# Second product of a SwiGLU FFN: seven block products in place of eight for 18 of its 22 tiles, with the gated blocks split early and kept in DRAM

## The chip, the core and the metric

The kernel runs on one core of a Trainium2 chip. Its time is the device time of one execution, in microseconds (us). Before the change the median of three runs is 1400.06 us (1399.25 to 1402.87). The engines that matter here are TensorE (PE in the rows), which multiplies matrices, VectorE (DVE), ScalarE (ACT), GpSimd (POOL) and SyncE (SP). GpSimd and SyncE are used here to issue transfers between SBUF (the memory on the core) and DRAM. PSUM is the small memory that TensorE writes; its banks hold 128 x 512 float32 values each.

## What is computed

A decoder block: attention and convolution branches, then a SwiGLU FFN. Only the FFN is touched:

```python
h2 = rmsnorm(x, norm2_g[l]) * (1.0 + sc2) + sh2
fg, fu = jnp.split(h2 @ w_ffn_in[l], 2, axis=-1)
x = x + gt2 * ((jax.nn.silu(fg) * fu) @ w_ffn_out[l])
return rmsnorm(x, final_g)
```

There are 1024 positions, 1024 channels and 2816 hidden channels, so the hidden side is 22 tiles of 128 channels. Everything is float32. To keep its accuracy on TensorE, each operand is split into a rounded high half and the remainder (the low half), and each product is made of three matmuls: high by high, high by low, low by high.

## The kernel before

**First product** (`h2 @ w_ffn_in`). The class `Pair` (line 1144) takes two hidden tiles at a time, first their gate columns, then their up columns, so that there are 22 pairs. A pair is a 2 x 2 by 2 x 2 block product made as seven products in place of eight (Winograd's form, table `PRODUCTS`): products 0 to 6 use the blocks A11, S1, S2, S4, S3, A12, A22 of the activations, where the S are sums and differences of blocks, and B11, T1, T2, B22, T3, B21, T4 of the weights, where T1 to T4 are differences. One product is 12 matmuls of 128 x 512 (4 tiles of depth, three matmuls each) into one of three PSUM banks: products 0, 2, 4, 6 go on adding into X, 1 and 3 into Z, 5 into Y. Between them the bank is read: after products 0, 1 and 2 ScalarE copies it out (`keep`: `kepta`, `keptc`, `keptb`), after 3, 4, 5 and 6 `out` makes the hidden tile from bank and kept copy, with VectorE for the additions and ScalarE for the silu of a gate pair. The next product into a bank waits until it has been read. There are six such banks, given out in turn.

**Weights.** `prepare` (line 1178) makes one product's weight block: for a T VectorE first takes the difference (`tt`), ScalarE rounds it (high half, `wb` or `wbp`), and VectorE takes the remainder (same tile). The loop at line 1386 prepares up to six products ahead (`LEAD`). In this stretch TensorE, VectorE and ScalarE each keep the order in which the code was written (`in_order`): an instruction that waits holds up everything behind it on its engine.

**Gated tiles.** A finished tile `g` (silu(gate) * up, 128 x 1024) goes to DRAM (`g_d`) by a transfer that GpSimd issues. There are 32 SBUF slots of 128 x 1024 for everything large; 28 hold the split blocks of the activations.

**Second product** (`@ w_ffn_out`). The gated tiles come in groups of 6, 6, 6 and 4 (line 1422). SyncE's queue loads them (`gl`), each is split (ACT 1024 columns, DVE 1024 columns), and for each of 8 output tiles m and each half of the positions the bank `fo` adds 3 matmuls per tile. VectorE then adds it, times a column, to the residual tile `x1r`. The last group of four also makes the final rmsnorm and the output.

Of the kernel before, what the change touches and what calls it, by code (L numbers as in the profile page):

```python
# [16 lines left out]
P = 128  # L17
S = 1024
# [53 lines left out]
LEAD = 6  # L72
CN = ((4, 0), (5, 0), (5, 1), (6, 0), (7, 0))
# [20 lines left out]
def tile_hybrid_block(ctx: ExitStack, tc: tile.TileContext, xT, vecs, cvec, lamv, relb, bsel, bmask, jrev,  # L94
# [793 lines left out]
    with tc.tile_pool(name="ps2", bufs=6, space=bass.MemoryType.PSUM) as ps2, ExitStack() as fxs:  # L888
# [203 lines left out]
        g_d = dp.tile([NFF, P, S], F32, name="g_d")  # L1092
        acts = {}
# [50 lines left out]
        class Pair:  # L1144
# [3 lines left out]

            def __init__(self, i):
                self.i = i  # L1150
                self.up = i % 2 == 1
                self.f = i // 2 * 2
                self.w, self.banks, self.kept = {}, {}, {}

            def load(self):
                self.raw = []
                for n in range(2):
                    if self.up:
                        t = fx[0].tile([P, D], F32, tag="raw", name="rawu", bufs=2)
                    else:  # L1160
                        t = wp.tile([P, D], F32, tag="wraw", name="rawg")
                    nc.sync.dma_start(t, w_fi[self.f + n + (NFF if self.up else 0)])
                    self.raw.append(t)
                (b11, b21), (b12, b22) = ((t[:, :HB], t[:, HB:]) for t in self.raw)
                self.b = dict(B11=b11, B21=b21, B12=b12, B22=b22)

            def source(self, name):
                b = self.b
                if name == "T1":
                    self.t = fx[0].tile([P, S], F32, tag="tt", name="tt", bufs=2)  # L1170
                if name[0] == "T":

                    b[name] = self.t[:, HB:] if name == "T3" else self.t[:, :HB]
# [7 lines left out]
            def high(self, p):  # L1181
# [3 lines left out]
                split_hi(w[:, :HB], src)  # L1185
                return w, src

            def low(self, part):
                w, src = part
                V.tensor_tensor(out=w[:, HB:], in0=src, in1=w[:, :HB].bitcast(F32), op=ALU.subtract)  # L1190

            def product(self, p, part=range(KH)):
                an, bn, x = self.PRODUCTS[p]
                if part[0] == 0:
# [5 lines left out]
                for k in part:  # L1200
                    a = acts[an][k]
                    ks = slice(k * P, (k + 1) * P)
                    ls = slice(HB + k * P, HB + (k + 1) * P)

                    mm3(self.banks[x], w[:, ks], w[:, ls], a[:, :HB], a[:, HB:], first and k == 0, k == KH - 1,
                        skip_group_check=not first)
# [37 lines left out]
            def store(self, n):  # L1244

                f = self.f + n
                if self.up and f < NFF - 2:
                    G.dma_start(g_d[f], hidden[f])
# [6 lines left out]
        nblock = [0]  # L1255

        def weight_block():
            n = nblock[0] % NWB
            nblock[0] += 1
            if n < NWB - 4:  # L1260
# [123 lines left out]
        late = {}  # L1384
        G0 = list(range(NFF - 6, NFF))
        for n, (g, p) in enumerate(order):
            if n < 14:
                continue
            if p == 1 and g.i + 2 < NFF:
# [183 lines left out]
```

## Time and profile before

| | before |
|---|---|
| median of three runs | 1400.06 us |
| profiled execution: its own time | 1404.03 us |
| profiled execution: span from first to last instruction | 1402.2 us |
| TensorE busy | 1360.9 us, 97% |
| VectorE busy | 964.4 us, 69% |
| ScalarE busy | 598.9 us, 43% |
| mean granted TensorE clock | 0.993 |
| moved by DMA | 135.10 MB |

Busy time is the sum over an engine's instructions. Matmuls overlap, so one matmul's own duration is longer than the distance between two starts, and it is the distance that adds up to the time. The chain of waits is followed backwards from the last instruction, at each step to what released it. In a row in order of time the idle time before an instruction stands in brackets with what ended it. In names, `<-` has the output at its left and the inputs at its right; a line such as L107 is that of a helper through which all engines' instructions run.

### The profile page before, as it was taken

Reading aid. Unit: us, or ns where it says so; the run is one execution under the profiler, and the core shown is the slowest. Engines: PE = TensorE matmul, PEld = TensorE weight load, DVE = VectorE, ACT = ScalarE, POOL = GpSimd, SP = SyncE. Lnnn points to the kernel's source line nnn. Section 1 sums busy time; section 2 is a strip of 40 time slices with the busy share of each in tenths; the row PEclk is TensorE's granted clock in tenths of the full one; section 3 lists DMA queues with packets and bytes.
Section 4 is the critical chain, followed back from the end, with each engine's and each line's share of the span. In section 5 each row is a group of like instructions: output and inputs, shape, how many; then the busy total and the mean of one; then the engine's idle time right before and its main releaser. Section 6 shows DMA issues by size and latency. Waiting matters only on the chain.

```text
span 1402.2 us, 15979 instructions
## 1 busy us (share of the span) xinstructions
PE 1360.9 (97%) x6178; PEld 1113.0 (79%) x6178; DVE 964.4 (69%) x1473; ACT 598.9 (43%) x974; POOL 45.3 (3%) x71
## 2 busy tenths in 40 slices
PE   7999999999999999999998999999999999999996
PEld 5678887877788887787766888888888888888886
DVE  7847788899989896887788655656555554434345
ACT  5546666666511115533565333333333332212145
POOL 0000000000000000000000000000000000000004
PEclk9999999999999999999999999999999999999998
DMA  8511011101111123339612222332222335313203
GB/s 296 194 31 34 30 43 30 31 16 38 40 59 46 45 91 105 120 132 324 211 38 103 86 105 98 120 120 91 90 75 78 111 128 191 135 45 113 72 15 121
DMA packets 44270, 135.10 MB, mean 96 GB/s; under 512 B 4857, under 2 KB 7841, under 8 KB 44194
## 3 DMA queue, kind: packets, MB, share of 16 engines
q1 hardware_dynamic: 39458, 118.88, 25.3%
q0 software_dynamic: 4160, 14.68, 3.1%
q8 instruction: 48, 0.79, 0.2%
q10 hardware_dynamic: 576, 0.52, 0.1%
q14 instruction: 28, 0.23, 0.1%
HBM read 115.19 MB, written 18.88 MB: 96 GB/s over the span
## 4 chain that ended last, share of the span: by engine, by line
PE 78%; DVE 9%; ACT 6%; DMA 4%; issue 1%; POOL 1%; SPq 0%; DVEq 0%; ACTq 0%; POOLq 0%
PE fx L107 16%; PE fo L119 16%; PE proj L107 8%; PE fz L107 8%; PE ga L107 5%; PE fy L107 4%; PE gc L107 4%; PE oa L107 3%; PE oc L119 3%; PE vacc L119 2%; DMA ada<-in_w_ada 2%; PE sc L107 2%; PE wo L119 2%; PE av L107 2%; PE wps L107 1%
## 5 line engine op out<-in xcount | busy, mean ns | idle before, releaser
L119 DVE SCALAR_TENSOR_TENSOR x1r<-fo,cols,x1r 128x512 f32<-128x512 f32 (+1 forms) x72 | 49.3, 690 | 119.9 <-PE fo L119 119.6
L119 PE MATMUL fo<-gl,wh_fo 128*128 128x512 f32 x288 | 112.2, 390 | 0.0
L119 PE MATMUL fo<-gh,wl_fo 128*128 128x512 f32 x288 | 112.1, 389 | 0.0
L119 PE MATMUL fo<-gh,wh_fo 128*128 128x512 f32 x288 | 111.9, 389 | 0.0
L107 DVE SCALAR_TENSOR_TENSOR cacc<-u,vec,cacc 128x1022 f32<-128x1022 f32 (+28 forms) x87 | 110.2, 1267 | 2.2
L107 PE MATMUL proj<-hhi,wh_in 128*128 128x512 f32 x239 | 99.3, 416 | 1.7 <-DVE kl L119 1.7
L107 PE MATMUL proj<-hhi,wl_in 128*128 128x512 f32 x240 | 94.9, 395 | 0.0
L107 PE MATMUL proj<-hlo,wh_in 128*128 128x512 f32 x240 | 94.6, 394 | 0.0
L107 PE MATMUL fx<-A,wb 128*128 128x512 f32 x335 | 80.9, 397 | 2.8 <-DVE g L107 2.8
L119 ACT ACTIVATE wh_fo<-wr_fo 128x768 fp32r<-128x768 f32 x24 | 20.3, 847 | 135.9 <-PE fo L119 130.3
L107 PEld LDWEIGHTS fx<-A,wb 128*128 128x128 f32 x335 | 63.9, 191 | 17.3 <-issue 3.7
L107 PE MATMUL fz<-S,wb 128*128 128x512 f32 x312 | 75.4, 390 | 1.6 <-DVE S L107 1.6
L107 PE MATMUL fx<-S,wb 128*128 128x512 f32 x312 | 75.2, 390 | 1.4 <-DVE S L107 1.3
L107 PEld LDWEIGHTS fz<-S,wb 128*128 128x128 f32 x312 | 58.4, 188 | 14.5 <-DVE S L107 2.4
L107 PEld LDWEIGHTS fx<-S,wb 128*128 128x128 f32 x312 | 58.5, 188 | 14.2 <-DVE S L107 1.6
L107 DVE TENSOR_TENSOR wb<-tt,wb 128x512 fp32r<-128x512 f32 x52 | 35.8, 693 | 45.2 <-ACT wb L107 45.1
L119 PEld LDWEIGHTS fo<-gl,wh_fo 128*128 128x128 f32 x288 | 54.1, 188 | 11.7 <-DVE gl L119 0.4
L119 PEld LDWEIGHTS fo<-gh,wh_fo 128*128 128x128 f32 x288 | 54.1, 188 | 11.3
L119 PEld LDWEIGHTS fo<-gh,wl_fo 128*128 128x128 f32 x288 | 54.1, 188 | 11.1
L119 ACT ACTIVATE e<-sc,mn 128x512 f32<-128x512 f32 (+7 forms) x64 | 47.2, 739 | 25.9 <-DVE mn L119 25.0
L107 ACT ACTIVATE wb<-tt 128x512 fp32r<-128x512 f32 x52 | 32.6, 629 | 59.5 <-DVE tt L107 59.3
L107 PEld LDWEIGHTS proj<-hhi,wh_in 128*128 128x128 f32 x239 | 45.7, 191 | 11.3 <-issue 3.6
(324 smaller groups left out, 3364.9 us busy)
## 6 DMA issues: line engine op xcount, KB each, us to landing
ada<-in_w_ada SPq DMA_DIRECT2D x32, 512.0 KB, 4.4
rawu<-in_w_fi SPq DMA_DIRECT2D x22, 512.0 KB, 3.5
rawg<-in_w_fi SPq DMA_DIRECT2D x22, 512.0 KB, 4.3
g_d<-g POOLq DMA_DIRECT2D x20, 512.0 KB, 4.1
gl<-g_d SPq DMA_DIRECT2D x20, 512.0 KB, 5.6
wr_fo<-in_w_fo SPq DMA_DIRECT2D x24, 384.0 KB, 3.1
adac<-in_w_ada SPq DMA_DIRECT2D x16, 512.0 KB, 4.8
wr_wo<-in_w_out SPq DMA_DIRECT2D x16, 512.0 KB, 5.2
```

Source lines behind the costliest of these rows:

```text
L107: self.last = f(*args, **kw)
L119: self.last = self.chain(f, *args, **kw) if self.chain else f(*args, **kw)
```

## The change

18 of the 22 gated tiles (`NST = 9` twos) no longer come into the second product as they are. While the first product goes on, `g_steps` makes from each two tiles the seven left-hand blocks of Winograd's form (A12, A22, A11, S1, S3, S2, S4): it splits each into high and low half in a tile `gst` and lets GpSimd store it in DRAM (`gs_d`). The steps of a two start at product 4 of its up pair and go on one per product, behind the matmuls and ahead of the reading of the bank, to product 3 of the next gate pair; those of the first two stand two per product at the start. In the second product these 18 tiles make three depths of 3 x 2 tiles, for each of which four `Group`s (a subclass of `Pair`, two output tiles each) make seven products of 9 matmuls. Their left-hand blocks are loaded by GpSimd's queue (`gb`, 21 per depth), 3 after each product of the last up pair and, for the later depths, 7 early and the rest as slots fall free. The weight blocks are prepared four products ahead. Each product is read out by VectorE into `x1r`. The four tiles that are left go as the last group did. The `ada2` loads, two in each 14 products, become one.

The core of the diff (the last group's code only moves to the left):

```diff
+LEAD2 = 4
+NST = 9
+GP = 3
+GB = ("A11", "S1", "S2", "S4", "S3", "A12", "A22")
...
-                if self.up and f < NFF - 2:
+                if self.up and f >= 2 * NST:
                     G.dma_start(g_d[f], hidden[f])
+        class Group(Pair):
+            n = GP * P
+            OUT = ((0, 0, "X"), (1, 1, "Z"), (0, 1, "X"), (0, 1, "Z"), (1, 1, "X"), (0, 0, "Y"), (1, 0, "X"))
...
+            def blocks(self, name):
+                return gacts[self.g][name]
+            def evacuate(self, p):
+                hf, n, x = self.OUT[p]
+                t = x1[self.m + n][:, hf_sl(hf)]
+                V.scalar_tensor_tensor(out=t, in0=self.banks[x], scalar=col(5, self.m + n), in1=t, op0=ALU.mult,
+                                       op1=ALU.add)
+        def g_steps(i):
+            a11, a21 = (hidden[2 * i][:, hf_sl(hf)] for hf in range(2))
+            a12, a22 = (hidden[2 * i + 1][:, hf_sl(hf)] for hf in range(2))
+            def put(name, src):
+                t = slot("gst", F32R)
+                split(t[:, :HB], t[:, HB:], src)
+                G.dma_start(gs_d[i * 7 + GB.index(name)], t)
+            def summed(name, out, x, y, op=ALU.subtract):
+                def f():
+                    t = out if out is not None else t2("gs1")
+                    V.tensor_tensor(out=t, in0=x, in1=y, op=op)
+                    put(name, t)
+                return f
+            return [lambda: put("A12", a12), lambda: put("A22", a22), lambda: put("A11", a11),
+                    summed("S1", None, a21, a22, ALU.add), summed("S3", a21, a11, a21), summed("S2", a11, a22, a21),
+                    summed("S4", a12, a12, a11)]
...
+        def fetch_blocks(group, n):
+            while n and wanted and wanted[0][0] == group:
+                n -= 1
+                g, name, k = wanted.pop(0)
+                if g == 1 and GP <= GP * ORDER.index(name) + k < GP + NWB - 6:
+                    t = fx[0].tile([P, D], F32R, tag="wb", name="gbw", bufs=NWB - 4)
+                else:
+                    t = slot("gb", F32R)
+                nc.gpsimd.dma_start(t, gs_d[(g * GP + k) * 7 + GB.index(name)])
+                gacts.setdefault(g, {}).setdefault(name, []).append(t)
...
+        late = g_steps(0)
         for n, (g, p) in enumerate(order):
...
             g.product(p)
+            if first:
+                if g.up and p == 4 and g.i // 2 < NST:
+                    late = g_steps(g.i // 2)
+                for _ in range(2 if n < 18 else 1):
+                    if late:
+                        late.pop(0)()
             g.evacuate(p)
...
+                if i == NFF - 1:
+                    fetch_blocks(0, GP)
+                    if p >= 5:
+                        x1r()
+            else:
+                if i < NFF + 4 and len(x1) < KD:
+                    x1r()
+                if g.m == 2 and p == 0:
+                    fetch_blocks(g.g + 1, 7)
+                elif g.m == KD - 2:
+                    fetch_blocks(g.g + 1, GP)
...
-        groups = [G0] + [list(range(a, b)) for a, b in ((0, 6), (6, 12), (12, 16))]
+        grp = list(range(2 * NST, NFF))
```

VectorE's order in the first product, in the middle of it, from the remainder of the next up pair's B11 to the first addition of the gate pair's product 3; first before the change. `wb` are remainders, `tt` are differences of weights, `g13` is a hidden tile.

```order
L107 TENSOR_TENSOR wb_7298<-rawu_7159,wb_7298 128x512
L107 TENSOR_TENSOR tt_7316<-rawu_7161,rawu_7159 128x512
L107 TENSOR_TENSOR wb_7318<-tt_7316,wb_7318 128x512
L107 ISA ada2_7219,cols_90<-ada2_7219,crow_82,bada_84 128x1024
L107 ISA cols_90 128x1
L107 TENSOR_TENSOR tt_7316<-rawu_7161,tt_7316 128x512
L107 TENSOR_TENSOR wb_7337<-tt_7316,wb_7337 128x512
L107 TENSOR_TENSOR g13_7352<-fz_7301,keptb_7333 128x512
```

The same place now; `g10` and `g11` are the two finished tiles, whose sums (written over them) and remainders (`gst`) stand between:

```order
L112 TENSOR_TENSOR wb_7459<-rawu_7306,wb_7459 128x512
L112 TENSOR_TENSOR g10_7266<-g10_7266 128x512
L112 TENSOR_TENSOR gst_7476<-g10_7266,gst_7476 128x512
L112 TENSOR_TENSOR tt_7482<-rawu_7308,rawu_7306 128x512
L112 TENSOR_TENSOR wb_7484<-tt_7482,wb_7484 128x512
L112 TENSOR_TENSOR g10_7266<-g11_7229,g10_7266 128x512
L112 TENSOR_TENSOR gst_7500<-g10_7266,gst_7500 128x512
L112 TENSOR_TENSOR tt_7482<-rawu_7308,tt_7482 128x512
L112 TENSOR_TENSOR wb_7507<-tt_7482,wb_7507 128x512
L112 TENSOR_TENSOR g11_7229<-g11_7229,g10_7266 128x512
L112 TENSOR_TENSOR gst_7523<-g11_7229,gst_7523 128x512
L112 TENSOR_TENSOR g13_7527<-fz_7462,keptb_7504 128x512
```

Behind each weight block stands a step of the gated tiles, a sum and a remainder, and the addition that reads product 3's bank (`fz`) comes behind all of them.

ScalarE's order at the same place before, from the copy of product 0's bank to the gate's silu:

```order
L107 ACTIVATE kepta_7292<-fx_7279 128x512
L107 ACTIVATE wb_7298<-rawu_7159 128x512
L107 ACTIVATE keptc_7314<-fz_7301 128x512
L107 ACTIVATE wb_7318<-tt_7316 128x512
L107 ACTIVATE keptb_7333<-fx_7279 128x512
L107 ACTIVATE wb_7337<-tt_7316 128x512
L107 ACTIVATE g13_7352<-g13_7352 128x512
```

And now, where the row ahead of `kepta` is the rounding of S1:

```order
L112 ACTIVATE gst_7449<-gs1_7447 128x512
L112 ACTIVATE kepta_7453<-fx_7434 128x512
L112 ACTIVATE wb_7459<-rawu_7306 128x512
L112 ACTIVATE gst_7476<-g10_7266 128x512
L112 ACTIVATE keptc_7480<-fz_7462 128x512
L112 ACTIVATE wb_7484<-tt_7482 128x512
L112 ACTIVATE gst_7500<-g10_7266 128x512
L112 ACTIVATE keptb_7504<-fx_7434 128x512
L112 ACTIVATE wb_7507<-tt_7482 128x512
L112 ACTIVATE gst_7523<-g11_7229 128x512
L112 ACTIVATE g13_7527<-g13_7527 128x512
```

Each copy of a bank (`kepta`, `keptc`, `keptb`) now stands behind the rounding of a gated block (`gst`), which needs the sum that VectorE takes in the same product.

SyncE's queue where the second product starts, before (`gl` gated tiles, `wr_fo` weights, `x1r` the residual):

```order
L177 DMA wr_fo00_8594<-in_w_fo 128x768
L177 DMA wr_fo01_8642<-in_w_fo 128x768
L1410 DMA gl16_8564<-g_d_3193 128x1024
L1410 DMA gl17_8566<-g_d_3193 128x1024
L1410 DMA gl18_8568<-g_d_3193 128x1024
L1410 DMA gl19_8570<-g_d_3193 128x1024
L177 DMA wr_fo02_8690<-in_w_fo 128x768
L177 DMA wr_fo03_8738<-in_w_fo 128x768
L1435 DMA x1r0_8592<-x1_d_3192 128x1024
L1435 DMA x1r1_8640<-x1_d_3192 128x1024
L1435 DMA x1r2_8688<-x1_d_3192 128x1024
```

And now (`rawu` and `rawg` are weights of the first `Group`s):

```order
L1284 DMA rawu_8769<-in_w_fo 128x768
L1284 DMA rawu_8771<-in_w_fo 128x768
L1284 DMA rawg_8964<-in_w_fo 128x768
L1474 DMA x1r0_8888<-x1_d_3192 128x1024
L1474 DMA x1r1_8913<-x1_d_3192 128x1024
L1474 DMA x1r2_8930<-x1_d_3192 128x1024
```

The first load of `x1r` now stands behind the load into `rawg_8964`, whose buffer falls free when the first `Group`'s T3 has been taken.

## Rows read from the trace of the kernel before

**Rows 1.** The page, part 1: busy us of each engine, share of span, instructions.

```profile
PE 1360.9 (97%) x6178; PEld 1113.0 (79%) x6178; DVE 964.4 (69%) x1473; ACT 598.9 (43%) x974; POOL 45.3 (3%) x71
```

**Rows 2.** Chain that ended last: start us, us, what; both products of the FFN.

```profile
844.15 2.72 PE fz L107 x12
...
1143.35 2.72 PE fx L107 x12
1146.08 222.21 PE fo L119 x996
```

**Rows 3.** Page, part 5, one of three alike: busy, mean ns of one, idle before.

```profile
L119 PE MATMUL fo<-gh,wh_fo 128*128 128x512 f32 x288 | 111.9, 389 | 0.0
```

**Rows 4.** Stretch: its us, then busy PE, PEld, DVE, ACT, POOL, PEclk, DMA, GB/s.

```profile
914.24:952.32 38.08, 38.08 (x169) 31.55 (x168) 23.55 (x36) 14.02 (x24) 1.06 (x3) 1.00 0.32 111
```

**Rows 5.** VectorE in order of time, first product: start us, us, instruction [idle before].

```profile
898.39 0.69 DVE L107 TENSOR_TENSOR tt<-rawu,tt 128x512 f32<-128x512 f32 x1
899.84 0.69 DVE L107 TENSOR_TENSOR wbp<-tt,wbp 128x512 fp32r<-128x512 f32 x1 [0.76 <-ACT wbp L107]
902.46 0.69 DVE L107 TENSOR_TENSOR wb<-rawg,wb 128x512 fp32r<-128x512 f32 x1 [1.93 <-ACT wb L107]
903.07 0.68 DVE L107 TENSOR_TENSOR tt<-rawg 128x512 f32<-128x512 f32 x1
...
907.06 0.69 DVE L107 TENSOR_TENSOR tt<-rawg,tt 128x512 f32<-128x512 f32 x1
...
909.47 0.69 DVE L107 TENSOR_TENSOR keptb<-fz,keptb 128x512 f32<-128x512 f32 x1 [0.34 <-PE fz L107]
910.20 0.69 DVE L107 TENSOR_TENSOR g<-keptb,g 128x512 f32<-128x512 f32 x1
```

**Rows 6.** ScalarE in the same stretch.

```profile
899.17 0.63 ACT L107 ACTIVATE wbp<-tt 128x512 fp32r<-128x512 f32 x1
901.31 0.60 ACT L107 ACTIVATE kepta<-fx 128x512 f32<-128x512 f32 x1 [1.51 <-PE fx L107]
901.80 0.62 ACT L107 ACTIVATE wb<-rawg 128x512 fp32r<-128x512 f32 x1
...
907.78 0.63 ACT L107 ACTIVATE wb<-tt 128x512 fp32r<-128x512 f32 x1 [0.43 <-DVE tt L107]
```

**Rows 7.** Chain again, third pair of the first product.

```profile
772.80 3.00 PE fz L107 x12
775.80 3.00 PE fx L107 x12
```

**Rows 8.** Transfers issued from 800 to 1143 us: KB each, median us to landing.

```profile
g_d<-g POOLq DMA_DIRECT2D x18, 512.0 KB, 4.1
...
x1r<-x_d SPq DMA_DIRECT2D x5, 512.0 KB, 6.8
```

**Rows 9.** Tile g_d, stores and loads: duration ns min/median/max; us to landing.

```profile
L1248 POOL DMA_DIRECT2D g_d<-g x20: 531/531/539, 758.8 to 1109.0; - x20
...
DMA to landing us min/median/max: 2.9/4.2/7.9
```

**Rows 10.** Stretches as in rows 4: fullest transfers, then behind the last products.

```profile
625.00:630.00 5.00, 5.00 (x24) 4.14 (x23) 4.41 (x7) 1.60 (x2) 0.73 (x1) 1.00 1.01 395
630.00:635.00 5.00, 5.00 (x24) 4.14 (x23) 4.11 (x8) 1.59 (x2) 0.55 (x1) 1.00 1.01 371
1388.00:1392.00 4.00, 1.51 (x10) 0.94 (x8) 2.65 (x6) 2.95 (x8) 4.00 (x6) 1.00 0.31 109
1392.00:1396.00 4.00, 1.96 (x5) 0.80 (x4) 0.79 (x2) 3.18 (x5) 2.09 (x3) 0.56 0.45 155
```

**Rows 11.** By form, from 1143 us: additions to x1r, splits of 768 columns.

```profile
L119 DVE SCALAR_TENSOR_TENSOR x1r<-fo,cols,x1r 128x512 f32<-128x512 f32 x56 | 42.0, 751 | 116.9 <-PE fo L119 116.7
...
L119 DVE TENSOR_TENSOR wl_fo<-wr_fo,wh_fo 128x768 fp32r<-128x768 f32 x22 | 20.9, 950 | 0.0
...
L119 ACT ACTIVATE wh_fo<-wr_fo 128x768 fp32r<-128x768 f32 x22 | 18.6, 848 | 135.9 <-PE fo L119 130.3 <-issue 5.5
```

More of the change, by code (lines that the diff above doesn't have):

```diff
@@ L1092, in tile_hybrid_block @@
         g_d = dp.tile([NFF, P, S], F32, name="g_d")
+        gs_d = dp.tile([NST * 7, P, S], F32R, name="gs_d")
         acts = {}
@@ L1382, in tile_hybrid_block, with x1r @@
         nprep = 17
-        late = {}
-        G0 = list(range(NFF - 6, NFF))
+        gacts = {}
+        x1 = []
+        ORDER = [a for a, b, x in Pair.PRODUCTS]
+        wanted = [(g, name, k) for g in range(NST // GP) for name in ORDER for k in range(GP)]
+        def fetch_blocks(group, n):
[8 more added lines that the diff above has]
+                gacts.setdefault(g, {}).setdefault(name, []).append(t)
+        def x1r():
+            x1.append(slot(f"x1r{len(x1)}"))
+            nc.sync.dma_start(x1[-1], x1_d[len(x1) - 1])
+        seq = pairs + [Group(i) for i in range(NST // GP * KD // 2)]
+        order += [(g, p) for g in seq[NFF:] for p in range(7)]
+        late = g_steps(0)
         for n, (g, p) in enumerate(order):
@@ new lines, in tile_hybrid_block, with fg, weighted, end @@
+        parts = (slice(0, HB), slice(HB, HB + HB // 2), slice(HB + HB // 2, S))
+        stf, accs, lasts, rest = {}, {}, {}, []
+        def fg(m):
+            return vec[:, O_FG + m:O_FG + m + 1]
+        def weighted(hs, m):
+            return hs != parts[-1] or m < KD - 2
+        def end(hs, engine):
+            sums = [accs[hs]] + (rest if hs == parts[-1] else [])
+            for i, t in enumerate(sums):
+                T.matmul(stf[hs], ones, t, start=(i == 0), stop=(i == len(sums) - 1))
+            r = rstd_from([stf[hs]], 1.0 / D, lasts[hs], fslot)[0]
+            for m in range(KD):
+                t = x1[m][:, hs]
+                if weighted(hs, m):
+                    engine.tensor_tensor(out=t, in0=t, in1=r, op=ALU.mult)
+                else:
+                    V.scalar_tensor_tensor(out=t, in0=t, scalar=fg(m), in1=r, op0=ALU.mult, op1=ALU.mult)
+                (nc.scalar if m % 2 and hs == parts[-1] else nc.sync).dma_start(outT[m][:, hs], t)
@@ new lines, in tile_hybrid_block @@
+        for i, hs in enumerate(parts):
+            nt = hs.stop - hs.start
+            stf[hs] = bankG("stf")[:, 0:nt]
+            one = hs != parts[-1]
+            for m in range(KD):
+                ps = bank("fo")[:, 0:nt]
+                gemm_cols(ps, wl[m], g_acts, hs)
+                if i and m == EP:
+                    end(parts[i - 1], G)
+                t = x1[m][:, hs]
+                V.scalar_tensor_tensor(out=t, in0=ps, scalar=col(5, m), in1=t, op0=ALU.mult, op1=ALU.add)
+                sq = (t2 if m else fslot)("sq")[:, 0:nt]
+                if one or m < KD - 1:
+                    sqi = A.activation(sq, t, AF.Square)
+                else:
+                    V.tensor_tensor(out=sq, in0=t, in1=t, op=ALU.mult)
+                if m == 0:
+                    accs[hs] = sq
+                elif one or m < KD - NL:
+                    V.tensor_tensor(out=accs[hs], in0=accs[hs], in1=sq, op=ALU.add)
+                else:
+                    rest.append(sq)
+                if m == (KD - 3 if one else KD - 2):
+                    lasts[hs] = sqi
+                if weighted(hs, m):
+                    A.activation(t, t, AF.Copy, scale=fg(m))
@@ L1509, in _bias_consts @@
+        end(parts[-1], V)
 def _bias_consts():
```

186 lines of the change are left out of this document (72 added, 114 removed).

## The prediction

> **What bounds the kernel now.** I read the page's part 1 first: TensorE is busy 97% of the span [rows 1]. Then the chain of waits: through both products of the FFN it is TensorE alone, product after product at 2.72 us for 12 matmuls, and 222.21 us of `fo` without a break [rows 2]; the matmuls of the second product have no idle time ahead of them [rows 3]. One matmul so costs 2.72 / 12 = 0.2267 us, and each one removed is worth that, as long as nothing makes TensorE wait. The reader should then ask what the cover is: in 14 products (a gate pair and an up pair, 38.08 us) VectorE is busy 23.55 us and ScalarE 14.02 [rows 4]. That looks like much room. The rows in order of time say how it is really used: VectorE takes a difference (898.39), ScalarE rounds it (899.17), VectorE takes the remainder (899.84), and in between VectorE stands idle 0.76 us, as its order is fixed [rows 5, 6].
>
> **What is removed.** 18 tiles x 8 output tiles x 2 halves x 3 = 864 matmuls become 3 depths x 4 groups x 7 products x 9 = 756. 108 fewer at 0.2267 is **-24.5 us**. The tail is the same. The splits of gated tiles and weights that go lay beside TensorE and give nothing.
>
> **The steps beside the first product.** A step is a rounding, a remainder (0.69 us) and a store, and four of seven have a sum (0.69) ahead. By busy time it fits: 23.55 + 11 x 0.69 = 31.1 of 38.08 us. By order it does not. From rows 5 and 6: the rounding starts 0.72 to 0.78 us behind the difference that it needs (907.06 to 907.78, 898.39 to 899.17; I take 0.76), the remainder 0.67 behind the rounding, the next instruction on VectorE 0.61 behind that (902.46 to 903.07). A sum or difference with its split holds VectorE's queue for 0.76 + 0.67 + 0.61 = 2.04 us. In a gate pair's products 0, 2 and 3 there are two, a weight's T and a gated sum: 4.08 us for a product of 2.72. What is queued behind them is the reading of the banks: ScalarE's copies stand behind the rounding of the gated block, and VectorE's additions behind its remainder; TensorE waits for both, two products later.
>
> I walk it, with time 0 at the start of a gate pair's product 0. The up pair's end is late already. Behind its product 4 VectorE's starts follow each other at 0.12 (a remainder still runs), two additions 0.73 and 0.61 (909.47 to 910.20, rows 5), T4 2.04, A22 0.61, two additions 0.73 and 0.61, B21's remainder 0.82 (A11's, behind it, waits for its rounding), A11's 0.61: the reading of product 6 starts at 6.88, and that product ended at 5.44. It is 1.44 late.
> - T from 2.05, S1's sum 4.09, its rounding 4.85, the copy of product 0's bank 0.52 behind it (901.31 to 901.80 is 0.49) and 0.60 long, to 5.97. Product 2 needs that bank, was due at 5.44 and starts at 6.01: **+0.57**.
> - B11 is rounded at 5.87, remainder 6.54, S3's sum 7.15, rounding 7.91, copy to 9.03; product 3 was due at 8.73, starts at 9.07: **+0.34**.
> - T 9.19, S2's sum 11.23, rounding 11.99, copy to 13.11; product 4 was due at 11.79, starts at 13.15: **+1.36**.
> - T 13.27, S4's sum 15.31, remainder 16.74, addition 17.35, silu 18.11, rounding of B22 18.63, remainder 19.30, addition for product 4's bank 19.91 to 20.60; product 6 was due at 18.59, starts at 20.64: **+2.05**.
>
> Sum 4.3 us. Behind it VectorE has one split a product or fewer and catches up before the next up pair's product 3. This repeats for eight twos of tiles: 8 x 4.3 = **+34.4 us**. The first two's seven steps stand in four products, with seven weight blocks: eight splits with a sum (16.3) and six without (0.61 each, 3.7) are 20.0 us for 10.9 of TensorE, 9.1 late, and then product 6's wait of 2.05: **+11.2 us** (9 to 14). The three short stalls of before there, 3.00 for 2.72 twice and a smaller one [rows 7], go under: **-0.6**.
>
> **Start of the second product.** From the end of product 0 of the last up pair (first three slots free) to product 6 of the first `Group` there are 6 x 2.72 + 6 x 2.04 = 28.6 us. In them must come 21 blocks of 0.524 MB, two `g` stores and two `x1r`: 13.1 MB; three more `x1r` and three weights stand in the same queue: 15.9 MB. The fullest stretches moved 395 and 371 GB/s [rows 10], mean 383. With 1.5 us for a lone transfer's start (2.9 us less 1.4 for its bytes, rows 9) this takes 35.7 to 43.0 us: 7.1 to 14.4 over, I take **+11**. The low end is 2.5: if nothing is crowded, only `x1r0` is late, issued some 1.3 us into the `Group` (one addition and a difference ahead of it), landing 4.1 to 6.8 later [rows 8], added in 0.75 [rows 11], while product 2 is due at 4.08. The high end is 18 (all eight `x1r` first). Each of the two later depths has 24.5 us for 14 blocks and four weights, 8.9 MB, which take 24.7: together **+1** (0 to 6). The Trainium skill (DMA: Bandwidth & Descriptors, Specifications) gives some 358 GB/s as one core's limit at HBM; the trace went beyond it in rows 10, so the sum goes by the rows; by the page these two would be +13 and +4.
>
> **Inside the `Group`s.** VectorE per `Group`: 384 columns are estimated at 0.56 us, ScalarE's 0.51, from 768 at 0.95 and 0.85 [rows 11] and 512 at 0.69 and 0.62 [rows 5, 6]. Four splits with difference 1.66 each, three at 0.48, seven additions at 0.67: 12.7 of 14.28 us, and the busiest product (2.33 for 2.04) is followed by a light one. I take 0, up to 5 for all twelve and the last four tiles' splits, which now stand there.
>
> **Clock.** Behind TensorE's last products the granted clock fell to 0.56 (of the levels 2.4 and 1.2 GHz mostly the lower) after a pause of some 2.5 us [rows 10]. The pauses of about 5 us at the first two tiles and at the first `Group` may do the same; a product at the lower level costs 2.0 to 2.7 more. I take **+2** (0 to 8).
>
> **Sum.** -24.5 + 34.4 + 11.2 - 0.6 + 11 + 1 + 2 = +34.5 us. Against the profiled execution's own 1404.03 that is 1438.5; the median lies 4 below that execution, and I forecast from it: **1434.6 us**.
>
> **Rivals.**
> - *Hidden after all.* If the copies of the banks came in time (VectorE's 31.1 us of 38.08 decide, not its order), -24.5 + 2.5 + 0 to 3 gives 1378 to 1382. For it: busy shares. Against it: the fixed order, in which VectorE idles for ScalarE at each split [rows 5]. It decides at a reading no later than one product (2.72 us) behind its bank's last matmul. 0.08; half hidden, 1385 to 1412, 0.08.
> - *Stores come late.* 28 of 32 slots hold activations, so a `gst` tile waits for the store two steps before. A11's rounding comes 5.4 us behind A12's store issue, S1's 6.0 behind A22's. 4.1 us to landing [rows 8] fits, but the range goes to 7.9 [rows 9], and there are now seven stores for two. At 6.8 (`x1r` among its like, rows 8) A11 is 1.4 late and so is all behind it: 8 x 1.4 to 2, and some 6 at the first two tiles, gives 1450 to 1460. 0.14.
> - *Forecast,* stalls as walked, 1412 to 1448: 0.70.
>
> **How the numbers follow.** Low ends (3.5 a cycle, 9, 2.5, 0, 0) sum to +14, 1414; stores late and a crowded start to +62, 1462. I give 1412 to 1462. A measurement of this kernel tells about 0.3% (4 us) from no change. Faster holds the first rival and the lower part of half hidden: 0.11. Within 0.3%: 0.04. Slower: 0.85.
>
> **What would show it.** In the profile after: TensorE idle in front of the gate pairs' products 2, 3, 4 (released by ScalarE's `kept` copies) and 6 (by VectorE's `g`), 4 to 4.5 us in each 14 products, and 11 at the third pair; a wait at the first `Group` for `gb` or for `x1r`; no idle time inside later `Group`s; 756 matmuls in `Group`s. It is wrong if the first product still runs at 38.08 us for 14 products, or if `gst` waits for DMA.

## The result: 1437.1 us, 2.6% slower

| | before | after |
|---|---|---|
| median | 1400.8 us (4 runs) | 1437.1 us (4 runs) |
| ratio after to before | | 1.0258, 95% interval 1.0240 to 1.0276 |
| profiled execution: own time, span | 1404.0, 1402.2 us | 1436.9, 1435.1 us |
| mean granted TensorE clock | 0.993 | 0.985 |

The kernel before has one more run here than the three of its section. Ratios compare runs in one state; of the six executions of `c2_best` below, one took 3442.4 us for no known reason and its ratio leaves that one out (with it the median is 1395.0 us, without it 1394.8).

The forecast was 1434.6 us in a range of 1412 to 1462. Part 1 of the page of the changed kernel (busy us of each engine, share of the span, instructions) answers to [rows 1]: TensorE has its 108 matmuls less and still a longer span, while VectorE has 225 instructions more.

```profile
PE 1350.5 (94%) x6070; PEld 1094.1 (76%) x6070; DVE 1070.8 (75%) x1698; ACT 637.7 (44%) x1079; POOL 104.1 (7%) x181
```

**The first product.** TensorE in order of time in the changed kernel, products 1 to 6 of a gate pair (start us, us, instruction, count, idle before and what ended it). Without waits the starts are 2.72 apart.

```profile
857.85 2.88 PE L112 MATMUL fz<-S,wb 128*128 128x512 f32 x12
861.22 3.03 PE L112 MATMUL fx<-S,wb 128*128 128x512 f32 x12 [0.49 <-ACT kepta L112]
864.26 3.03 PE L112 MATMUL fz<-S,wb 128*128 128x512 f32 x12
868.30 3.02 PE L112 MATMUL fx<-S,wbp 128*128 128x512 f32 x12 [1.00 <-ACT keptb L112]
871.15 2.88 PE L112 MATMUL fy<-A,wbp 128*128 128x512 f32 x12
875.75 5.78 PE L112 MATMUL fx<-A,wbp 128*128 128x512 f32 x24 [1.71 <-DVE g L112]
```

The distances exceed 2.72 by 0.65 ahead of product 2, 0.32 ahead of 3, 1.32 ahead of 4, 0.13 ahead of 5 and 1.88 ahead of 6; the first product after that pays 0.16 more, 4.46 in all. From product 6 at 833.21 to the next gate pair's product 6 at 875.75 there are 42.54 us, against 38.08 in [rows 4].

What makes the third of these waits, in order of time on VectorE, ScalarE and TensorE in the same kernel:

```profile
864.37 0.69 DVE L112 TENSOR_TENSOR tt<-rawu 128x512 f32<-128x512 f32 x1
...
865.09 0.63 ACT L112 ACTIVATE wb<-tt 128x512 fp32r<-128x512 f32 x1 [0.88 <-DVE tt L112]
865.75 0.69 DVE L112 TENSOR_TENSOR wb<-tt,wb 128x512 fp32r<-128x512 f32 x1 [0.70 <-ACT wb L112]
866.36 0.69 DVE L112 TENSOR_TENSOR g<-g,g 128x512 f32<-128x512 f32 x1
867.13 0.63 ACT L112 ACTIVATE gst<-g 128x512 fp32r<-128x512 f32 x1 [1.41 <-DVE g L112]
867.66 0.58 ACT L112 ACTIVATE keptb<-fx 128x512 f32<-128x512 f32 x1
867.79 0.69 DVE L112 TENSOR_TENSOR gst<-g,gst 128x512 fp32r<-128x512 f32 x1 [0.74 <-ACT gst L112]
868.30 0.50 PE L112 MATMUL fx<-S,wbp 128*128 128x512 f32 x1 [1.00 <-ACT keptb L112]
...
868.40 0.69 DVE L112 TENSOR_TENSOR tt<-rawu,tt 128x512 f32<-128x512 f32 x1
```

Difference, rounding, remainder, sum, rounding, remainder: from 864.37 to the next difference at 868.40 this is one chain of 4.03 us (2 x 2.02) for a product of 2.72, in which VectorE and ScalarE take turns and TensorE has no part. The copy `keptb`, which TensorE waits for, is behind the second rounding. Over the eight cycles VectorE waits for ScalarE like this (from the waits of the changed kernel, 790.69 to 1130.85: us in total, times, longest):

```profile
DVE wb L112 <- ACT wb L112: 45.9, 57, 1.5
DVE wbp L112 <- ACT wbp L112: 32.5, 39, 1.5
DVE gst L112 <- ACT gst L112: 24.1, 33, 0.7
```

That is 102.5 us. The row of the stretch (columns as in [rows 4]) has VectorE busy for 231.38 of 340.16 us:

```profile
790.69:1130.85 340.16, 314.36 (x1345) 249.75 (x1345) 231.38 (x359) 143.67 (x249) 29.77 (x56) 1.00 0.42 147
```

231.4 + 102.5 is 333.9 of 340.2 us, at a busy share of 68%. But this sum alone does not make VectorE the bound. In the same eight cycles of the kernel before, where TensorE is busy throughout, it is 180.3 + 106.2 = 286.5 of 304.7 us:

```profile
DVE wb L107 <- ACT wb L107: 62.3, 57, 1.9
DVE wbp L107 <- ACT wbp L107: 43.9, 40, 1.9
```

```profile
781.36:1086.07 304.71, 304.71 (x1345) 252.48 (x1345) 180.32 (x274) 112.27 (x194) 8.50 (x16) 1.00 0.29 97
```

Some of these waits are slack: ScalarE itself first waits for TensorE (1.51 us ahead of `kepta` at 901.31 in [rows 6]), and VectorE's 1.93 us at 902.46 in [rows 5] lie behind that. What tells the two kernels apart is the chain of 4.03 us in a product of 2.72, where the kernel before has at most one split with a difference, 2.04 us by [rows 5, 6].

**The first two tiles.** The stretch goes from product 6 of the first two pairs to product 6 of the next gate pair. TensorE at its start and at its longest wait in the changed kernel, and then at its start in the kernel before:

```profile
756.35 8.43 PE L112 MATMUL fx<-A,wb 128*128 128x512 f32 x36 [2.81 <-DVE g L112]
...
776.17 5.49 PE L112 MATMUL fz<-S,wbp 128*128 128x512 f32 x12 [4.86 <-ACT keptc L112]
```

```profile
757.26 10.05 PE L107 MATMUL fx<-A,wb 128*128 128x512 f32 x36 [2.83 <-DVE g L107]
```

Behind the wait of 4.86 us twelve matmuls took 5.49 us for 2.88, at a granted clock of 0.50. The kernel before lost clock too, at the start: 0.66 in the first 5 us, and 10.05 us for 8.43.

**The start of the second product.** Order of time, TensorE, VectorE and SyncE (SPq), at the first `Group`, and then three stretches:

```profile
1192.28 0.33 SPq L1284 DMA_DIRECT2D rawg<-in_w_fo  x1
...
1192.66 2.56 SPq L1474 DMA_DIRECT2D x1r<-x_d  x5
1192.90 2.20 PE L112 MATMUL fz<-gb,wbp 128*128 128x512 f32 x9
...
1202.51 0.75 DVE L112 SCALAR_TENSOR_TENSOR x1r<-fx,cols,x1r 128x512 f32<-128x512 f32 x1 [9.14 <-DMA x1r<-x_d]
...
1203.37 4.18 PE L112 MATMUL fx<-gb,wb 128*128 128x512 f32 x9 [8.27 <-issue]
```

```profile
1193.00:1198.00 5.00, 2.10 (x10) 1.41 (x8) 0.37 (x1) 0.19 (x1) 1.73 (x4) 1.00 1.11 410
1198.00:1203.00 5.00, 0.00 (x0) 0.00 (x0) 0.49 (x1) 0.00 (x0) 1.07 (x2) 0.55 1.06 365
1203.00:1208.00 5.00, 4.63 (x11) 3.70 (x12) 2.92 (x6) 0.94 (x2) 1.07 (x2) 0.50 1.06 411
```

VectorE waits 9.14 us for `x1r0`, and TensorE 8.27 us behind it. Then the granted clock is at 0.50, the lower level (1.2 GHz), and the next nine matmuls take 4.18 us for the 2.20 of the nine at 1192.90. From the first product of the twelve `Group`s to the last there are 181.0 us (1190.86 to 1371.90); without a wait they would be 12 x 14.28 - 2.04 = 169.3. The first `Group` took 25.29 us for 14.28; the other eleven are 0.7 us over in all.

**The whole difference of the spans,** 32.9 us, by stages: the FFN starts 0.9 earlier; first two tiles 34.3 for 24.1, **+10.2**; eight cycles 340.2 for 304.6 (8 x 38.08), **+35.5**; the rest, 304.3 for 316.2, **-11.9**, which is -24.5 for the matmuls and +12.6 for the start and what follows.

### The profile page after: what moved, and what is told of

Read it like the earlier page. It is cut to its first block, busy times and chain, and to the rows that moved or that the text cites. A ratio compares the mean times of both kernels' runs of the same rounds, so it can differ in the third digit from the quotient of the medians.

```text
span 1435.1 us, 16435 instructions
## 1 busy us (share of the span) xinstructions
PE 1350.5 (94%) x6070; PEld 1094.1 (76%) x6070; DVE 1070.8 (75%) x1698; ACT 637.7 (44%) x1079; POOL 104.1 (7%) x181
## 5 line engine op out<-in xcount | busy, mean ns | idle before, releaser
L112 ACT ACTIVATE wbp<-tt 128x512 fp32r<-128x512 f32 (+1 forms) x66 | 38.1, 579 | 131.3 <-DVE tt L112 110.8
L112 ACT ACTIVATE wb<-tt 128x512 fp32r<-128x512 f32 (+1 forms) x68 | 41.1, 606 | 94.3 <-DVE tt L112 77.9
L112 DVE TENSOR_TENSOR wb<-tt,wb 128x512 fp32r<-128x512 f32 (+1 forms) x68 | 44.7, 660 | 48.0 <-ACT wb L112 47.9
L112 DVE TENSOR_TENSOR wbp<-tt,wbp 128x512 fp32r<-128x512 f32 (+1 forms) x66 | 41.3, 627 | 48.1 <-ACT wbp L112 48.1
L112 PE MATMUL fx<-gb,wbp 128*128 128x512 f32 x282 | 68.6, 390 | 0.1
L112 ACT ACTIVATE gst<-g 128x512 fp32r<-128x512 f32 x54 | 33.9, 629 | 69.1 <-DVE g L112 42.9
L112 PE MATMUL fx<-S,wbp 128*128 128x512 f32 x216 | 53.8, 396 | 8.2 <-ACT keptb L112 4.6
L112 PEld LDWEIGHTS fx<-gb,wbp 128*128 128x128 f32 x282 | 52.8, 188 | 11.5 <-DMA gb<-gs_d 0.5
L112 PE MATMUL fz<-S,wbp 128*128 128x512 f32 x216 | 55.2, 406 | 6.4 <-ACT keptc L112 4.9
L112 PEld LDWEIGHTS fx<-S,wbp 128*128 128x128 f32 x216 | 39.7, 188 | 21.4 <-ACT keptb L112 6.6
```

Source lines behind the costliest of these rows:

```text
L112: self.last = f(*args, **kw)
```

## The experiments

The *order theory* says that the fixed order of VectorE and ScalarE makes the 45.7 us of the first product. Its rivals are the amount of work on VectorE and ScalarE (work theory), the transfers (transfer theory), and, for the second product, what the first `Group` really waits for. The ratios are to runs of the kernel before on the same chip, whose medians were 1401.5 to 1403.4 us beside the experiments. For every kernel the table has the eight cycles (product 6 to product 6, from the order of time on TensorE) and the `Group`s (first product to last).

| kernel | eight cycles, us | over 304.6 | `Group`s, us | median, us | ratio to before (95%) |
|---|---|---|---|---|---|
| changed | 340.2 | 35.5 | 181.0 | 1437.1 | 1.0258 (1.0240 to 1.0276) |
| e1_read_first | 334.7 | 30.0 | 181.0 | 1432.0 | 1.0206 (1.0171 to 1.0240) |
| e2_second_only | 304.8 | 0.1 | 181.3 | 1387.5 | 0.9887 (0.9865 to 0.9908) |
| e3_no_stores | 340.5 | 35.8 | 180.7 | 1434.9 | 1.0224 (1.0201 to 1.0247) |
| e4_no_sums | 304.8 | 0.2 | 180.2 | 1398.3 | 0.9970 (0.9954 to 0.9986) |
| e5_x1r_apart | 340.2 | 35.6 | 182.9 | 1439.8 | 1.0258 (1.0230 to 1.0286) |
| e6_staged | 325.7 | 21.1 | 180.6 | 1418.8 | 1.0110 (1.0089 to 1.0131) |
| e7_pool_sums | 331.7 | 27.0 | 180.8 | 1424.9 | 1.0156 (1.0132 to 1.0181) |
| c1_all | 329.3 | 24.7 | 182.6 | 1424.0 | 1.0157 (1.0135 to 1.0179) |
| e8_own_buffer | 311.8 | 7.2 | 181.2 | 1408.4 | 1.0037 (1.0018 to 1.0056) |
| c2_best | 307.3 | 2.7 | 185.2 | 1395.0 | 0.9927 (0.9902 to 0.9953) |
| e9_hold | 340.0 | 35.4 | 180.1 | 1436.4 | 1.0242 (1.0218 to 1.0265) |
| c3_hold | 309.4 | 4.7 | 180.3 | 1393.0 | 0.9930 (0.9910 to 0.9950) |

**e2_second_only: the second product alone.**

```diff
-                    late = g_steps(g.i // 2)
+                    late = []
...
-                nc.gpsimd.dma_start(t, gs_d[(g * GP + k) * 7 + GB.index(name)])
+                nc.gpsimd.dma_start(t, w_ada[len(wanted) % 6, k].bitcast(F32R))
```

(and no steps for the first two tiles either).

> The changed kernel without any step in the first product: no blocks are summed, split or stored, and the second product loads its blocks from a weight array of the same size instead (so its result is not the reference's). Order theory and work theory alike: the waits of the first product go whole, 35.8 in eight cycles and 10.1 in the first two tiles, and what is left is the second product with its start: 1437.1 - 45.9 = 1391, between 1385 and 1394, that is 6 to 15 under the kernel before. If the second product by blocks were itself the loss: 1400 or more.

1387.5 us, 1.1% under the kernel before. The first product is back at 304.8 us for eight cycles. The second product is a gain, with its late start (181.3 us, the same as in the changed kernel): the loss is the steps.

**e3_no_stores: the steps without their stores.**

```diff
-                G.dma_start(gs_d[i * 7 + GB.index(name)], t)
```

(The second product loads its blocks from a weight array, as in e2.)

> The changed kernel with every sum and split of the blocks, but none of the 63 stores; the second product loads its blocks from a weight array of the same size (so its result is not the reference's). Order theory and work theory: the stores cost next to nothing, since a new block's buffer waited for one for 3.6 us in the whole program: 1437 less 0 to 4, 1433 to 1438. Transfer theory (148 GB/s beside the products, or buffers that come free late, make the waits): most of the 46 us come back, 1391 to 1410.

1434.9 us, and the eight cycles are as long as in the changed kernel (340.5). The transfer theory falls for the first product.

**e4_no_sums: the steps without the four sums.**

```diff
-                    t = out if out is not None else t2("gs1")
-                    V.tensor_tensor(out=t, in0=x, in1=y, op=op)
-                    put(name, t)
+                    put(name, x)
```

> The changed kernel with the four sums of each pair of tiles left out, 36 VectorE instructions of 0.69 us: the S blocks are split from an unsummed tile (so the result is not the reference's); all 63 splits, stores and loads stay. Order theory: each of these sums stands ahead of a rounding that the remainder behind it waits for, in the four products before the waits at 2, 4 and 6, and a delay is handed from product to product; without them the chain of each product is 0.69 shorter and most of the waits fall away, more than the sums' own 36 x 0.69 = 25 us: 1400, between 1392 and 1408. Work theory: the sums are 2.8 of the 7.6 us that VectorE has more in a cycle (4 sums and 7 remainders), 36% of 46 us: 1437 - 17 = 1420, between 1412 and 1426.

1398.3 us. The row of its eight cycles has TensorE busy throughout:

```profile
788.22:1093.03 304.81, 304.81 (x1344) 252.44 (x1345) 210.73 (x328) 144.49 (x250) 29.77 (x56) 1.00 0.47 164
```

VectorE has 20.7 us less work than in the changed kernel (231.4 to 210.7), and 35.3 of the 35.5 us come back, where the share in proportion (36%) would have been 13. So the changed kernel stands just beyond what its order can take. VectorE waits 87.3 us for the weights' roundings here, 298.0 of 304.8 us with its work, and TensorE does not notice. Less work and shorter chains come together here, so this run alone does not tell order from amount; the next ones do.

**e1_read_first: the reading ahead of the step.**

```diff
             g.product(p)
+            g.evacuate(p)
             if first:
...
-            g.evacuate(p)
```

> The changed kernel with one line moved: in each product the bank is read (and g formed from it) before the step of the block split, not after it. The same instructions on the same engines. Order theory: what costs the 46 us of the first product is the place of the steps in the fixed order; with the readings ahead of the steps the waits before products 2 and 4 (0.49 and 1.00 in a cycle of the changed kernel, some 0.3 more at each restart, 2.1 in all) go in 8 cycles, less in the first two tiles; the wait before product 6 stays or grows, since the weight's own split now stands behind the whole step. 1437 - 8 x 1.5 - 2 = 1423, between 1415 and 1430. Work theory (VectorE and ScalarE simply have too much to do beside the products): nothing changes, 1437 within 3.

1432.0 us (1426.1 to 1437.2): 5 us for the 14 expected. The interval of its ratio only just touches the changed kernel's; in the traces the eight cycles are 5.5 us shorter. TensorE in two cycles of this kernel:

```profile
864.99 3.01 PE L112 MATMUL fx<-S,wbp 128*128 128x512 f32 x12 [0.32 <-ACT keptb L112]
...
873.12 5.74 PE L112 MATMUL fx<-A,wbp 128*128 128x512 f32 x24 [2.40 <-DVE g L112]
...
914.69 7.34 PE L112 MATMUL fx<-A,wb 128*128 128x512 f32 x24 [2.39 <-DVE g L112]
```

The wait ahead of product 2 is gone and that ahead of 4 is down from 1.00 to 0.32, as expected. The wait ahead of 6 rose from 1.71 to 2.40: the whole delay now ends there. In two of eight cycles (914.69 here) the product behind it ran slower too, 7.34 for 5.74. This suggests, and does not show, that the place of the reading matters little while two chains of 2 us stand in one product.

**e6_staged: the same instructions, no remainder right behind its rounding.**

```diff
+            for f in waiting:
+                f()
+            waiting = []
+            for total, high, low in steps:
+                total()
+            for w, part in parts:
+                w.low(part)
             g.product(p)
+            g.evacuate(p)
+            for total, high, low in steps:
+                high()
+                waiting.append(low)
```

> The changed kernel with the same instructions in an order in which no VectorE instruction of a step stands right behind the ScalarE rounding that it needs: in each product first the difference of the weights, then the remainder of the last product's block, then this product's sum, then the remainder of the weights, then the matmuls and the reading of the bank, and the rounding of the block last, behind the kept copy. Order theory: VectorE has 28.9 us of work in a cycle of 38.08 without waits, so most of the 4.46 a cycle goes, to 1 at most, and half of the first two tiles' 10: 1437 - 8 x 3.6 - 5 = 1403, between 1395 and 1410. Work theory: the same work on the same engines, 1437 within 5.

1418.8 us. The same work in another order gives 14.4 of the 35.5 us back, which the work theory excludes; but not the 28.8 expected. What is late next stands in ScalarE's waits over the eight cycles of this kernel, and at one place in order of time:

```profile
ACT gst L112 <- DMA gs_d<-gst: 21.7, 18, 2.6
```

```profile
941.34 0.63 ACT L112 ACTIVATE gst<-gs 128x512 fp32r<-128x512 f32 x1 [2.15 <-DMA gs_d<-gst]
...
942.00 0.69 DVE L112 TENSOR_TENSOR gst<-gs,gst 128x512 fp32r<-128x512 f32 x1 [1.30 <-ACT gst L112]
```

A rounding now waits for a free slot, that is for the landing of an earlier store; in the whole of the changed kernel these waits are

```profile
ACT gst L112 <- DMA gs_d<-gst: 3.6, 2, 3.1
```

A block that is rounded one product before its remainder holds its slot 2.7 us longer, and there are only four slots beside the 28 of the activations.

**e8_own_buffer: the staged order with a buffer of its own for the blocks.** One weight buffer is given to them. The main lines that differ from e6:

```diff
-NWB = 10
+NWB = 9
+NGST = 1
...
-                    box["t"] = slot("gst", F32R)
+                    box["t"] = slot("gst", F32R) if GB.index(name) in (5, 0, 4, 3) else fx[0].tile([P, S], F32R, tag="gst", name="gst", bufs=NGST)
```

> The staged order with one weight buffer less (nine for ten) and that buffer given to the block splits, which use it for four blocks of each seven; the other three stay in the common slots. Buffer theory: the staged order still lost 2.8 us a cycle (122.65 us for three cycles from product 6 to product 6), because a rounding waited for a free slot, that is for an earlier store to land (1.45, 2.15 and 0.73 us in one cycle); with one buffer more these waits go, and with them the pauses and slower matmuls behind them: 1418.8 - 8 x 2.4 = 1400, between 1394 and 1408. Rival: the sums and remainders crowd VectorE in the seven products of the steps, whatever the buffers: 1414 to 1420. One weight buffer less may cost up to 4 in the first tile.

(The own buffer takes three blocks of seven, A22, S1 and S2, not four.) 1408.4 us, at the edge of what the buffer theory gave. The eight cycles fall to 311.8 us, and the wait is half of what it was:

```profile
ACT gst L113 <- DMA gs_d<-gst: 10.4, 8, 2.7
```

Order and buffer together take 28.3 of the 35.5 us, the order alone 14.4. A buffer more in the old order was not run; there is little for it to take, as slots make ScalarE wait 3.6 us there and leaving out the stores (e3) gained nothing.

**e7_pool_sums: the sums on GpSimd.**

```diff
-                    V.tensor_tensor(out=t, in0=x, in1=y, op=op)
+                    G.tensor_tensor(out=t, in0=x, in1=y, op=op)
```

> The changed kernel with its 36 sums on GpSimd in place of VectorE, in the same places of the program, nothing else moved. Without any sums the waits of the first product were gone but for the first two tiles (1398). Order theory: GpSimd waits for nothing but the tiles and so runs ahead of the rounding; its sum takes about 1.4 us (the 128x512 product on GpSimd at the end of the kernel), which hides: 1398 plus 0 to 12, 1405. Rival: GpSimd's sum and the hand-over to ScalarE stand in the chain with 1.4 in place of 0.69, or slow VectorE beside them, and nothing is won: 1430 or more.

1424.9 us, between the two and nearer the rival. In order of time, GpSimd's sums and VectorE beside them:

```profile
900.74 1.63 POOL L1312 TENSOR_TENSOR g<-g 128x512 f32<-128x512 f32 x1
...
901.36 1.56 DVE L112 TENSOR_TENSOR gst<-gs,gst 128x512 fp32r<-128x512 f32 x1 [0.15 <-ACT gst L112]
...
902.45 3.32 POOL L1312 TENSOR_TENSOR g<-g,g 128x512 f32<-128x512 f32 x2
902.84 1.77 DVE L112 TENSOR_TENSOR wb<-rawu,wb 128x512 fp32r<-128x512 f32 x1
...
904.53 1.78 DVE L112 TENSOR_TENSOR gst<-g,gst 128x512 fp32r<-128x512 f32 x1
...
906.24 0.68 DVE L112 TENSOR_TENSOR tt<-rawu 128x512 f32<-128x512 f32 x1
```

While GpSimd's sums run in these rows, VectorE's 0.69 become 1.56 to 1.78. What VectorE no longer sums it loses beside GpSimd: it is busy 236.4 us in the eight cycles, 231.4 in the changed kernel. The Trainium skill (SBUF — State Buffer, Who interferes with whom) says that a VectorE instruction with two inputs in SBUF contends with a GpSimd instruction that reads SBUF; the trace agrees.

**e5_x1r_apart: the first two `x1r` early, the others later.**

```diff
+                    if p in (4, 5):
+                        x1r(nc.gpsimd)
                     fetch_blocks(0, GP)
-                    if p >= 5:
-                        x1r()
...
-                if i < NFF + 4 and len(x1) < KD:
-                    x1r()
+                if g.g == 0 and p in (2, 4) and len(x1) < KD:
+                    x1r(nc.sync, V.last.ins)
```

> The changed kernel with other loads of the residual tiles x1r: the first two on the GpSimd queue during the last tile of the first product, ahead of blocks and of no weight load, the other six one after the other during the first three Groups, each held until VectorE has reached its product. First-tile theory: the pause of 8.27 us in the second product's start is VectorE's first reading, which stood 9.14 us for the first x1r, because that load was issued at 1192.66 behind a weight load and shared 410 GB/s with four more x1r of 512 KB each; with it gone and the slower clock behind it gone too, some 8 of the start's 11 us come back: 1429, between 1426 and 1433. Block theory (the 22 blocks of 512 KB, 11.5 MB or 28 us at 410 GB/s from 1172.96 on, set the start, and the x1r only land beside them): 0 to 2 us come back, 1435 to 1438.

1439.8 us, no gain; the `Group`s take 182.9 us, 1.9 more. The pause is not gone, it is spread. TensorE at the first `Group` of this kernel:

```profile
1202.35 3.17 PE L112 MATMUL fz<-gb,wb 128*128 128x512 f32 x9 [3.85 <-issue]
...
1213.10 1.12 PE L112 MATMUL fx<-gb,wbp 128*128 128x512 f32 x3 [1.58 <-DMA gb<-gs_d]
1215.35 5.42 PE L112 MATMUL fx<-gb,wbp 128*128 128x512 f32 x12 [1.13 <-DMA gb<-gs_d]
```

`x1r0` no longer makes VectorE wait, `x1r1` does for 5.64 us, and then two blocks are late. Here what came first only chose what was late, and the first-tile theory's 8 us are not found. But it was not tried well: in GpSimd's order the two loads left at 1189.44 and 1191.57, at most 3.2 us ahead of the 1192.66 of the changed kernel. c2_best and c3_hold below issue them 12 to 15 us ahead of the first `Group` and one block earlier still; there VectorE waits for no `x1r`, and the first two `Group`s take 36.8 and 37.2 us for the changed kernel's 39.6 and e5's 40.7. So early loads of two `x1r` and a block together give back 2.4 to 2.8 of the 11 us, and blocks are late behind them.

**e9_hold: the second depth's blocks held back.**

```diff
                 if g.m == 2 and p == 0:
-                    fetch_blocks(g.g + 1, 7)
+                    with tc.issue_after(V.last.ins):
+                        fetch_blocks(g.g + 1, 7)
```

> The changed kernel with the early loads of the second group's blocks (seven of 512 KB) held until VectorE has done the first Group's last reading; nothing else moved. Queue theory: at the start of the second product the transfers run at 400 to 415 GB/s from 1175 on, and what counts is which bytes are asked for ahead of those that are waited for; three of the held blocks were issued at 1196.53, 1198.54 and 1200.74, while VectorE waited for the first x1r until 1202.5: 1.57 MB, 3.8 us at 415 GB/s, some 1.5 to 3.8 of the pause of 8.27 go, 1437 - 3 = 1434, between 1432 and 1436. Rival: the first x1r, on another queue, is served ahead of them anyway, or the held blocks are missed at the second group: 1436 to 1441.

1436.4 us. The hold did not hold: it orders the issue and is no wait, and the instructions stand in the same order on every engine. The blocks left as in the changed kernel, ahead of even the first reading, at 1201.98, which waited for `x1r0`; GpSimd in order of time:

```profile
1196.78 0.54 POOL L1469 DMA_DIRECT2D gbw<-gs_d  x1 [0.80 <-issue]
...
1198.88 0.54 POOL L1469 DMA_DIRECT2D gb<-gs_d  x1 [1.57 <-DMA gb<-gs_d]
...
1201.31 0.54 POOL L1469 DMA_DIRECT2D gb<-gs_d  x1 [1.90 <-DMA gb<-gs_d]
```

The run is a second measurement of the changed kernel and tells nothing of the theories. The loads that e5 and the combinations hold are held in the same way, so there too only their place in the order changed.

**c1_all, c2_best, c3_hold: together.** c1_all is e5, e6 and e7 in one. c2_best leaves the sums on VectorE, takes e8's buffer, and orders each product as: difference, sum, both roundings, the weights' remainder, the matmuls, the reading, the block's remainder. The first two tiles have one step per product like the others. One block is loaded early into the own buffer, and the first two `x1r` are issued at products 2 and 3. c3_hold uses the own buffer in the second depth again.

> The staged order, the sums on GpSimd and the x1r loads apart, all three together on the changed kernel. If the parts add: the waits of the eight cycles (35.8) go whole, of the first two tiles' 10 some 5, of the start some 8: 1437 - 35.8 - 5 - 8 = 1388, between 1383 and 1396, under the kernel before. If something else takes their place (the doubled steps of the first tiles, the blocks' landings): 1397 or more.

> All that helped together: per product the difference of the weights, the sum, the remainder of the weights, the matmuls, the reading of the bank, the remainder of the block, with both roundings one behind the other on ScalarE; one own buffer for the blocks; one step in each product of the first two tiles too; the first two x1r on the GpSimd queue three products before the end of the first product, the other six held; one block loaded early into the own buffer. If the waits are what these changes take: at or under the kernel without any steps (1387.5), less 2 to 5 for the start: 1384, between 1378 and 1393, 0.7 to 1.7% under the kernel before. If a new wait takes their place: 1394 or more.

> The last combination with the same hold of the second group's blocks, and with its own block buffer used again in the second group, where the combination had one buffer less than the changed kernel and waited 0.47, 0.96 and 1.65 us for blocks. Queue theory: of the 5.4 us that the start still waited for blocks (1.89 and 3.49) some 3 go, of the 3.1 us of the later waits most: 1395 - 3 - 2.5 = 1389, between 1385 and 1393. Rival: the held blocks come late for the second group and the waits move there: 1394 or more.

c1_all is 1424.0 us; GpSimd's sums slow VectorE as in e7 (of its differences the 17 `tt<-rawu` take 1.30 us in the mean, the others 0.69). c2_best is 1395.0 us, 0.7% under the kernel before, but 2 us over the range expected. Its eight cycles:

```profile
780.23:1087.52 307.29, 305.58 (x1345) 252.02 (x1344) 230.59 (x363) 143.03 (x251) 30.91 (x58) 1.00 0.48 166
```

VectorE does the same work as in the changed kernel, 230.6 us to 231.4, in 307.3 us for 340.2. The first two tiles take 23.5 us (756.75 to 780.23) for 34.3. That settles the first product: 32.9 of the 35.5 us, and the first two tiles' 10.2, go with another order of the same work, one buffer more for the blocks and, in the first tiles, one step per product. What the buffer does in this order was not run apart; ScalarE still waits 17.0 us for landings, and TensorE waits only 1.8 us in all. But its `Group`s rose to 185.2 us. c3_hold mends that to 180.3 and comes to 1393.0; between the two the intervals overlap. In c3_hold the start still waits for blocks:

```profile
1165.51 1.50 PE L113 MATMUL fx<-gb,wbp 128*128 128x512 f32 x3 [1.94 <-DMA gb<-gs_d]
1169.66 6.57 PE L113 MATMUL fx<-gb,wbp 128*128 128x512 f32 x15 [2.66 <-DMA gb<-gs_d]
```

What is waited for at the start is shown, the `x1r` in the changed kernel and blocks here. Which bytes could be left for later is open, as a true wait was not tried.

## The prediction, point by point

- **Removed matmuls, -24.5:** 6178 to 6070 are the 108.
- **Steady cycles, +34.4:** +35.5. The walk gave 0.57, 0.34, 1.36 and 2.05 ahead of products 2, 3, 4 and 6; the starts are late by 0.65, 0.32, 1.32 and 1.88. What it left out is some 0.15 to each restart (12 matmuls in 3.02 for 2.88). Its reason held: the bank readings wait behind chains of 2.04 us (2.02 in the rows above), and another order of the same work takes the waits away (c2_best).
- **First two tiles, +11.2 - 0.6:** +10.2. Eight products without waits would be 21.8 us; the changed kernel was 12.6 over, 2.6 of it the product at the lower clock (5.49 for 2.88), which stood in another term. The kernel before was 2.3 over, not 0.6: 1.6 of that were its 36 matmuls with a granted clock of 0.66 at their start, which the prediction did not see.
- **Start, depths and clock, 11 + 1 + 2:** 12.6 in this stage, 11.0 of it in the first `Group` and 0.4 at the second depth. But of the 11.0 only some 8.4 are the wait, for a term of 11; 2.6 are slower matmuls behind it, which with the first tiles makes 5.2 for the clock's 2. That a transfer would be waited for was right, and the rate was near (410, 365 and 411 GB/s in the stretches above for 383); that the bytes asked for set the length of the wait is argued, not shown. The sum had no row for which transfer it would be: it was `x1r0`, behind the weight load.
- **Rival "hidden after all":** fell in the kernel as written. VectorE's work can be hidden, but in another order: in c2_best TensorE waits 1.8 us in eight cycles. The rival's 1378 to 1382 had 2.5 for the start; with the 12.6 of the changed kernel it would be 1388 to 1392, next to the 1393.0 of c3_hold.
- **Rival "stores come late":** fell for the changed kernel (e3; `gst` waited for DMA 3.6 us in all, twice). It came true in e6, where slots are held longer.
- **What was not foreseen:** that the order was so near to fitting that leaving out four sums frees all, and that a better order meets the four slots next.

Between the two profiled executions the change is 32.9 us, for +34.5 in the sum; between the medians it is 36.3, as the profiled execution of the kernel before was 3.2 us above its median, and so the forecast lies 2.5 under the median. The steady cycles are right by their mechanism. That the other terms come this near in sum has luck in it: the wait at the start was 2.6 too high and the clock 3.2 too low, and what the kernel before lost at its first tiles was missed.

## What to carry to other kernels

A busy share does not tell whether an engine has room, and busy time plus waits for a partner does not either: it was 94% of the eight cycles in the kernel before, which lost nothing. Follow the chain through both engines product by product and hold it against the product's length: 4.03 us for 2.72 was too long. Work that is split between two engines in a fixed order wants its next piece between the two halves; in e6 that held slots longer, so count the buffers with the order. When a stretch is full of transfers, loading one thing a little earlier can make another one late (e5).

## What the runs showed of the hardware

- **VectorE beside GpSimd:** a 128x512 remainder from SBUF took 1.56 to 1.78 us for 0.69 while GpSimd summed (e7), and GpSimd's sums took 1.52 to 1.59 in the mean for the 1.40 expected.
- **Transfers:** the five-microsecond stretches shown here ran at 365 to 411 GB/s, and one of c2_best (1140 to 1145) at 419. The Trainium skill (Perfetto Trace Analysis, Roofline) says that 358 GB/s is a core's share when both cores of a pair are active, and that one core alone can go beyond it, to about 435; the trace agrees that it goes beyond 358 (419), 435 was not reached, and no run here has a second core at work.
- **Stores beside the products** landed in 2.9 us in the median, at 147 GB/s in all, for the 4.1 of [rows 8].
- **The clock behind a pause:** in e6_staged a pause of 2.09 us ahead of product 6 (909.08) was followed by 24 matmuls in 7.33 us, a longer one of 2.64 (951.69) by 24 in 5.74. The granted clock of the 5 us behind the first was 0.66, behind the second 1.00. Ahead of the first two tiles a pause of 2.83 us cost clock in the kernel before (0.66) and one of 2.81 in the changed kernel did not (1.00). Why is open. In the changed kernel none of the pauses of 1.7 us ahead of product 6 of the eight cycles cost clock; in e1, e6 and c1 some pauses of 2.1 to 3.1 us did, 1.6 us each.
